# From residual rows to features between layers: VectorE block transposes and a DRAM scratch tile in place of TensorE transposes

## The chip, the cores and the metric

The kernel runs on one core of one Trainium2 chip. The metric is the device time of one execution in microseconds (us); the median of three runs is compared. The core has five engines with a queue of instructions each, which run at the same time: TensorE (PE; its weight loads are PEld), VectorE (DVE), ScalarE (ACT), GpSimd (POOL) and SyncE (SP). Sixteen DMA engines move data for the queues of SP, ACT and POOL.

## What is computed

A decoder trunk of four layers over a sequence of 256 rows of 2048 float32 values. Every layer normalizes the residual stream x, multiplies it with one wide input matrix, runs a mixer (latent attention, sparse attention, sliding window, latent attention) and a cross attention over a memory, gates the result and adds its output product to x.

```python
for i in range(DEPTH):                      # 4
    h = _rmsnorm(x, norm_in[i])             # x (1, 256, 2048)
    ...                                     # self_out, mq, gate from h @ w_in
    mem_out = _memory_attention(mq, mem_n @ w_mem_kv[i])
    y = jnp.concatenate([self_out, mem_out], axis=-1) * jax.nn.silu(gate)
    x = x + y @ w_out[i]
return _rmsnorm(x, final_norm)
```

## The kernel before, in words

The residual stream stays on chip as `xc`: four chunks `c` of 512 columns, each as two tiles `t` of 128 rows. Every product is made from float32r parts: a value is split into a high part (its rounding, made by ScalarE in `copy_act`, L74) and a low part (the rest, made by VectorE, L83), and three matmuls (high by high, high by low, low by high) are summed. Weights come by SP's DMAs into five tiles `wr`; `parts_of` splits them into `wh` and `wl`, of which there are three buffers each. So the split of a k-step (128 rows of a weight matrix) waits until the k-step three places earlier has been multiplied. I call these steps kv0 to kv15 in the product that opens layers 1 and 2 (`acc_kv`, 512 columns wide) and kva0 to kva15 in the one that opens layer 3 (`acc_kva`, 288 columns wide). Each step is six matmuls.

The last `w_out` of a layer (L1247) makes the four chunks one after the other: 24 matmuls (`acc_wo`), the addition into `xc` (L1251), and, where it is the last part, `nxt.chunk(c)` (L364) for the layer that follows. `chunk` makes `xT`, the features of this chunk on the partitions, in high and low parts, and the sums of squares of its rows (L234, ScalarE, into a scratch tile `junk`). In `to_features` (L211) TensorE turns four 128x128 pieces of each row tile into a PSUM bank (L215), VectorE multiplies them by the norm's weights into `xg` (L217), ScalarE and VectorE split `xg` into `xT`. Steps 4c to 4c+3 of the next layer's first product read chunk c of `xT`. There are three such boundaries: after layer 0 (some 935 to 970 us), after layer 1 and after layer 2 (some 1920 to 1955 us). Scratch tiles of 128x512 values (`tmp`: `xg`, `junk` and others) share four buffers.

The instructions of each engine run in one fixed order, which a scheduler with its own estimate of times sets when the program is built; a few are held in program order. POOL's queue carries the memory keys and values (`mv`, `mkT`), the bias tables and, in layers 0 and 1, one copy of a bias table at the first chunk of each of eight `w_out` calls (`not_before`, L175, a small copy named `tick`, then `table_copies`, L170).

Of the kernel before, what the change touches and what calls it, by code (L numbers as in the profile page):

```python
# [8 lines left out]
F32 = mybir.dt.float32  # L9
# [3 lines left out]
OP = mybir.AluOpType  # L13
AX = mybir.AxisListType

P = 128
# [29 lines left out]
def kernel(ctx: ExitStack, tc: tile.TileContext, a: dict, out: bass.AP,  # L46
                             kinds=(0, 1, 2, 0)):
    nc = tc.nc
# [3 lines left out]
    act = ctx.enter_context(tc.tile_pool(name="act", bufs=1))  # L52
    wk = ctx.enter_context(tc.tile_pool(name="wk", bufs=1))
    ps = ctx.enter_context(tc.tile_pool(name="ps", bufs=1, space=bass.MemoryType.PSUM))
    dr = ctx.enter_context(tc.tile_pool(name="dr", bufs=1, space=bass.MemoryType.DRAM))

    def misc(name, dt=F32):
        return ps.tile([P, 512], dt, name=name, tag="mp", bufs=4)

    def tmp(name, n=512, dt=F32):  # L60
        return wk.tile([P, n], dt, name=name, tag=f"t{n}", bufs=4)
# [5 lines left out]
    def f32(ap):  # L67
        return ap.bitcast(F32)
# [4 lines left out]
    def copy_act(o, i, scale=1.0):  # L73
        inst = nc.scalar.activation(o, i, AF.Copy, scale=scale)  # L74
        if pinned:
            tc.keep_in_program_order(inst)
# [4 lines left out]
    def split(hi, lo, src):  # L81
        copy_act(hi, src)
        nc.vector.tensor_sub(lo, src, f32(hi))  # L83


    xc = cst.tile([P, 4, 2, 512], F32, name="xc")
# [8 lines left out]
    gvec = cst.tile([P, P], F32, name="gvec")  # L95
    tc.keep_in_program_order(nc.scalar.dma_start(gvec, a["l_norms"]))

    class Features:

        def __init__(self, src, c):  # L100
            self.q = act.tile([P, 4, S], F32, name="ft", tag="pq", bufs=PQ)
            self.src = src[:, 4 * c:4 * c + 4, :]
# [108 lines left out]
    def to_features(dst, t, src, gcol, n=4):  # L211

        tp = misc("tp")
        for j in range(n):
            nc.tensor.transpose(tp[:, j * P:(j + 1) * P], src[:, j * P:(j + 1) * P], ident)  # L215
        xg = tmp("xg")
        nc.vector.tensor_mul(xg[:, :n * P].rearrange("p (j c) -> p j c", j=n),  # L217
                             tp[:, :n * P].rearrange("p (j c) -> p j c", j=n),
                             gvec[:, gcol:gcol + n][:, :, None].to_broadcast([P, n, P]))
        sl = slice(t * P, (t + 1) * P)  # L220
        g3 = xg[:, :n * P].rearrange("p (j c) -> p j c", j=n)
        split(dst[:, 0, :n, sl], dst[:, 1, :n, sl], g3)
# [9 lines left out]
    def square_sum(col, src):  # L232
        junk = tmp("junk")
        return nc.scalar.activation(junk[:, :src.shape[-1]], src, AF.Square, accum_out=col)  # L234
# [120 lines left out]
        nc.vector.tensor_add(dst[:, 1], z, pair[:, :, 1, :])  # L355


    class Norm:
        def __init__(self, layer):
            self.layer = layer  # L360
# [3 lines left out]
        def chunk(self, c):  # L364
            q = act.tile([P, 2, 4, S], F32R, name="xT", tag="xT", bufs=4)
            self.at.append(q)
            for t in range(2):
                src = xc[:, c, t, :]
                to_features(q, t, src, 64 + self.layer * 16 + c * 4)
                square_sum(self.ss[:, t * 4 + c:t * 4 + c + 1], src)  # L370

        def first_chunk(self, c):

# [958 lines left out]
```

## Time and profile before

| what | us |
|---|---|
| median of 3 runs | 2544.02 (2543.21 to 2544.23) |
| span of the profiled execution, first to last instruction | 2541.7 |
| TensorE busy in it | 2532.3 |
| VectorE, ScalarE, GpSimd busy | 1889.8, 1600.9, 95.6 |

The runs' times hold the span and the little that lies around it; the page gives the profiled execution's span only, 2.3 us under the median. Busy time is the time in which an engine had an instruction under way. A row of a timeline gives the start, the time until the end (rows of one kind in a row are merged), the engine, the line and the tiles, and in brackets how long the engine stood idle before and what ended that. The end of an instruction overlaps the start of the next, so starts are compared with starts.

### The profile page before, as it was taken

The numbers are of one execution on the slowest core, as the hardware profiler recorded it, in microseconds if no ns is written. First come the engines' busy times: TensorE is split into PE (matmuls) and PEld (weight loads), VectorE is DVE, ScalarE is ACT, GpSimd is POOL, SyncE is SP. The second block draws the span as 40 slices with busy tenths as digits, with TensorE's granted clock in tenths as the row PEclk, the third lists the DMA queues.
The fourth block names the chain that finished last, engine by engine and source line by source line (L and its number), as shares of the span: only waits on it lengthen the run. The fifth ranks groups of instructions, "written<-read, shape, count | busy, mean of one in ns | idle before, by whom it ended". The sixth has DMA issues, their size and how long they took to land.

```text
span 2541.7 us, 41606 instructions
## 1 busy us (share of the span) xinstructions
PE 2532.3 (100%) x14070; PEld 2185.3 (86%) x14070; DVE 1889.8 (74%) x3832; ACT 1600.9 (63%) x3291; POOL 95.6 (4%) x237
## 2 busy tenths in 40 slices
PE   9999999999999999999999999999999999999998
PEld 8888898888888889888888888888889888888887
DVE  6666667677777677988787777877867777777766
ACT  6556556566566566777666566667756666656655
POOL 1200000000000000000000000000000000000000
PEclk9999999999999999999999999999999999999999
DMA  9887777676667666766666565655656768676765
GB/s 315 260 262 257 248 215 236 169 191 176 187 194 207 195 197 188 219 190 175 190 187 182 174 216 175 182 176 177 195 158 178 225 189 218 194 194 183 222 173 183
DMA packets 479030, 511.67 MB, mean 201 GB/s; under 512 B 70720, under 2 KB 391616, under 8 KB 478176
## 3 DMA queue, kind: packets, MB, share of 16 engines
q1 hardware_dynamic: 462304, 451.82, 60.6%
q0 software_dynamic: 15792, 56.22, 7.0%
q8 instruction: 110, 1.80, 0.3%
q10 hardware_dynamic: 720, 0.98, 0.1%
q14 instruction: 104, 0.85, 0.1%
HBM read 483.67 MB, written 29.46 MB: 202 GB/s over the span
## 4 chain that ended last, share of the span: by engine, by line
PE 99%; DVE 1%; issue 0%; DMA 0%; ACT 0%; SPq 0%; ACTq 0%; DVEq 0%
PE acc_wo L292 20%; PE acc_g L313 14%; PE acc_g L317 7%; PE acc_mv L292 7%; PE acc_q L313 5%; PE acc_mq L313 5%; PE acc_mk L313 5%; PE acc_cq L313 4%; PE acc_qn L313 4%; PE acc_q L317 2%; PE acc_mq L317 2%; PE acc_mk L317 2%; PE acc_cq L317 2%; PE acc_qr L313 2%; PE acc_qn L317 2%; PE acc_va L292 2%
## 5 line engine op out<-in xcount | busy, mean ns | idle before, releaser
L74 ACT ACTIVATE wh<-wr 128x512 fp32r<-128x512 f32 (+1 forms) x1712 | 1062.6, 623 | 820.3 <-PE acc_g L313 147.3
L83 DVE TENSOR_TENSOR wl<-wr,wh 128x512 fp32r<-128x512 f32 (+1 forms) x1712 | 1155.1, 679 | 558.2 <-ACT wh L74 529.7
L313 PE MATMUL acc_g<-xT,wh 128*128 128x512 f32 x1536 | 483.8, 397 | 0.0
L292 PE MATMUL acc_wo<-wh,y 128*128 128x512 f32 x1504 | 473.2, 391 | 0.0
L317 PEld LDWEIGHTS acc_g<-xT,wl 128*128 128x128 f32 x1536 | 282.4, 188 | 63.0 <-DVE wl L83 1.1
L292 PEld LDWEIGHTS acc_wo<-wh,y 128*128 128x128 f32 x1504 | 282.5, 188 | 55.9
L317 PE MATMUL acc_g<-xT,wl 128*128 128x256 f32 x1536 | 304.8, 280 | 0.1
L292 PE MATMUL acc_wo<-wl,y 128*128 128x512 f32 x752 | 297.7, 396 | 0.0
L313 PEld LDWEIGHTS acc_g<-xT,wh 128*128 128x128 f32 x1536 | 235.4, 189 | 0.9
L292 PEld LDWEIGHTS acc_wo<-wl,y 128*128 128x128 f32 x752 | 141.3, 188 | 26.3
L313 PE MATMUL acc_q<-xT,wh 128*128 128x512 f32 x512 | 161.4, 396 | 0.0
L313 PE MATMUL acc_mq<-xT,wh 128*128 128x512 f32 x512 | 161.1, 396 | 0.0
L313 PE MATMUL acc_mk<-mT,wh 128*128 128x512 f32 x512 | 160.7, 395 | 0.0
L292 PE MATMUL acc_mv<-wh,mT 128*128 128x512 f32 x512 | 156.7, 390 | 0.0
L313 PE MATMUL acc_qn<-cT,wh 128*128 128x512 f32 x384 | 121.0, 396 | 0.0
L313 PE MATMUL acc_cq<-xT,wh 128*128 128x512 f32 x384 | 120.9, 396 | 0.0
L317 PEld LDWEIGHTS acc_mk<-mT,wl 128*128 128x128 f32 x512 | 95.8, 188 | 22.6 <-DVE wl L83 0.2
L1251 DVE TENSOR_TENSOR xc<-xc,acc_wo 128x1024 f32<-128x1024 f32 x92 | 112.0, 1218 | 2.6 <-PE acc_wo L292 2.3
L317 PEld LDWEIGHTS acc_q<-xT,wl 128*128 128x128 f32 x512 | 94.7, 188 | 22.2 <-issue 0.7
L317 PEld LDWEIGHTS acc_mq<-xT,wl 128*128 128x128 f32 x512 | 94.8, 188 | 21.7 <-issue 0.2
L292 PEld LDWEIGHTS acc_mv<-wh,mT 128*128 128x128 f32 x512 | 96.4, 189 | 19.8
L317 PE MATMUL acc_q<-xT,wl 128*128 128x256 f32 x512 | 102.2, 281 | 0.0
(332 smaller groups left out, 3830.7 us busy)
## 6 DMA issues: line engine op xcount, KB each, us to landing
wr<-in_w_out_dram SPq DMA_DIRECT2D x188, 512.0 KB, 3.7
wr<-in_w_in_a_dram SPq DMA_DIRECT2D x176, 512.0 KB, 4.3
wr<-in_w_mem_kv_dram SPq DMA_DIRECT2D x125, 512.0 KB, 4.5
wr<-in_w_in_b_dram SPq DMA_DIRECT2D x116, 512.0 KB, 3.6
wr<-in_w_in_c_dram SPq DMA_DIRECT2D x104, 512.0 KB, 3.5
wr<-in_w_uq_dram SPq DMA_DIRECT2D x288, 128.0 KB, 2.8
wr<-in_w_in_a_dram SPq DMA_DIRECT2D x32, 288.0 KB, 3.2
mv<-mv POOLq DMA_DIRECT2D x16, 512.0 KB, 5.9
```

The costliest lines, as they stand in the source:

```text
L74: inst = nc.scalar.activation(o, i, AF.Copy, scale=scale)
L83: nc.vector.tensor_sub(lo, src, f32(hi))
L292: nc.tensor.matmul(acc[t][:, :n], q[:, v, (s + k) % 4, t * P:(t + 1) * P], w_[:, :n], start=s + k == 0 and v == 0 and w_ is wh, stop=s + k ...
L313: nc.tensor.matmul(acc[j], wh[:, o:o + P], q[:, :, kt % 4, :], start=kt == 0, stop=False)
L317: nc.tensor.matmul(acc[j][:, 0, :], wl[:, o:o + P], q[:, 0, kt % 4, :], start=False, stop=kt == kts - 1)
L1251: nc.vector.tensor_add(xs, xs, acc)
```

## The change

`Norm.chunk` no longer calls `to_features`. VectorE transposes the 32x32 blocks of each row tile (`turn_blocks`, one instruction of 128x512 per tile) into scratch tiles `xet`; two DMAs on POOL's queue write them (256 KB each) to a DRAM tile `turned`; four more, one per group of 32 partitions, 128 KB each in runs of 512 bytes, read them back into `xt` with each feature's row whole. ScalarE and VectorE then make `xT` from `xt` in four pieces of 128x256, with the norm's weight as a factor per partition. The sums of squares come after that in program order. `xt` uses the buffers `big0` to `big3`. The first layer's features (`first_chunk`) and the latent mixer's use of `to_features` stay.

```diff
+    def turn_blocks(et, m0, src, step=1):
+        n = src.shape[-1] // P
+        nc.vector.transpose(et[:, :, m0:m0 + step * (n - 1) + 1:step, :],
+                            src.rearrange("p (m j c) -> p j m c", j=4, c=32))
+
+    def across(dst, ets):
+        u, n = len(ets), ets[0].shape[-1] // 4
+        d = dr.tile([u, 4, 32, 4, n], F32, name="turned", tag=f"turned{u * n}", bufs=4)
+        for t, et in enumerate(ets):
+            nc.gpsimd.dma_start(d[t].rearrange("i p j n -> (i p) (j n)"), et)
+        for j in range(4):
+            nc.gpsimd.dma_start(dst[32 * j:32 * j + 32].rearrange("p (i n) -> p i n", n=n),
+                                d[:, :, :, j, :].rearrange("t i p n -> p (t i) n"))
...
         def chunk(self, c):
             q = act.tile([P, 2, 4, S], F32R, name="xT", tag="xT", bufs=4)
             self.at.append(q)
+            ets = [tmp("xet") for t in range(2)]
             for t in range(2):
-                src = xc[:, c, t, :]
-                to_features(q, t, src, 64 + self.layer * 16 + c * 4)
-                square_sum(self.ss[:, t * 4 + c:t * 4 + c + 1], src)
+                turn_blocks(ets[t].rearrange("p (j m c) -> p j m c", j=4, m=4), 0, xc[:, c, t, :])
+            xt = act.tile([P, 8, 4, 32], F32, name="xt", tag=f"big{c}")
+            across(xt.rearrange("p u m c -> p (u m c)"), ets)
+            for k in range(4):
+                g = gvec[:, 64 + self.layer * 16 + c * 4 + k:][:, :1]
+                src = xt[:, :, k, :]
+                hi, lo = (q[:, v, k, :].rearrange("p (u c) -> p u c", c=32) for v in range(2))
+                copy_act(hi, src, scale=g)
+                nc.vector.scalar_tensor_tensor(lo, src, g, f32(hi), op0=OP.mult, op1=OP.subtract)
+            for t in range(2):
+                square_sum(self.ss[:, t * 4 + c:t * 4 + c + 1], xc[:, c, t, :])
```

The change moves instructions on ScalarE. At the boundary after layer 0 its queue had this order before, from the first square sums on (`wh<-wr` is the split of one k-step's weights, `xT<-xg` half of a chunk's features; the first row ends with the first k-step of the third chunk of `w_out`):

```order
L74 ACTIVATE wh<-wr 128x512 x20
L234 ACTIVATE junk,xss<-xc 128x512 x2
L74 ACTIVATE xT<-xg 128x4x128
L74 ACTIVATE wh<-wr 128x512
L74 ACTIVATE xT<-xg 128x4x128
L74 ACTIVATE wh<-wr 128x512 x3
```

These rows repeat for each of the four chunks, so that chunk 0 is split before the second k-step of the third chunk of `w_out`. In the changed kernel the same place reads, from the split of the third chunk's four k-steps of `w_out` on:

```order
L74 ACTIVATE wh<-wr 128x512 x4
L234 ACTIVATE junk,xss<-xc 128x512 x2
L74 ACTIVATE wh<-wr 128x512 x4
L234 ACTIVATE junk,xss<-xc 128x512 x2
L74 ACTIVATE wh<-wr 128x512 x3
L74 ACTIVATE xT<-xt,gvec 128x256 x4
L74 ACTIVATE wh<-wr 128x512
L74 ACTIVATE xT<-xt,gvec 128x256 x4
L74 ACTIVATE wh<-wr 128x512
L234 ACTIVATE junk,xss<-xc 128x512
L74 ACTIVATE wh<-wr 128x512
L234 ACTIVATE junk,xss<-xc 128x512
L74 ACTIVATE wh<-wr 128x512 x5
L74 ACTIVATE xT<-xt,gvec 128x256 x4
```

The first `x4` splits are the third chunk of `w_out`, the second `x4` the fourth, the `x3` after them kv0 to kv2. The first four pieces of `xT` now stand behind the split of kv2, the next four behind kv3, the third four behind kv6 to kv10; the last four, not shown, come behind kv11.

At the boundary after layer 2 ScalarE's queue in the changed kernel reads, from the split of the fourth chunk of `w_out` on (`wh<-wr 128x288` is the split of one step kva):

```order
L74 ACTIVATE wh<-wr 128x512 x4
L74 ACTIVATE xT<-xt,gvec 128x256 x4
L74 ACTIVATE wh<-wr 128x288
L234 ACTIVATE junk,xss<-xc 128x512
L74 ACTIVATE wh<-wr 128x288
L234 ACTIVATE junk,xss<-xc 128x512
L74 ACTIVATE wh<-wr 128x288 x3
L234 ACTIVATE junk,xss<-xc 128x512 x2
L74 ACTIVATE wh<-wr 128x288 x2
L74 ACTIVATE xT<-xt,gvec 128x256 x4
L74 ACTIVATE wh<-wr 128x288 x2
L74 ACTIVATE xT<-xt,gvec 128x256 x4
```

Chunk 0 stands ahead of kva0, chunk 1 behind kva6, chunk 2 behind kva8; the last four pieces, not shown, stand behind kva14.

POOL's queue had nothing between the first and the last of the following rows before. Now it reads, between the loads of memory keys and the small copy with which the next layer begins:

```order
L659 DMA mkr<-mkT_127 128x1024
L369 DMA turned<-xet 128x512 x2
L371 DMA xt<-turned 32x8x128 x4
L369 DMA turned<-xet 128x512 x4
L371 DMA xt<-turned 32x8x128 x8
L369 DMA turned<-xet 128x512 x2
L371 DMA xt<-turned 32x8x128 x4
L177 COPY tick<-kr 128x1
```

The writes of chunks 1 and 2 stand together ahead of the reads of both, and the writes of chunk 3 behind those reads; after layer 1 it is the same, with two small fills ahead of the last four reads. After layer 0 the writes and reads go by pairs of chunks (four writes, eight reads, twice), behind a copy of a bias table.

## Rows read from the trace of the kernel before

**Rows 1.** Page, parts 1, 2 and 4: busy time; clock by slice; chain by engine.

```profile
PE 2532.3 (100%) x14070; PEld 2185.3 (86%) x14070; DVE 1889.8 (74%) x3832; ACT 1600.9 (63%) x3291; POOL 95.6 (4%) x237
...
PEclk9999999999999999999999999999999999999999
...
PE 99%; DVE 1%; issue 0%; DMA 0%; ACT 0%; SPq 0%; ACTq 0%; DVEq 0%
```

**Rows 2.** Timeline of PE in `w_out`, without and with the transposes.

```profile
919.70 0.39 PE L292 MATMUL acc_wo<-wl,y 128*128 128x512 f32 x1
919.92 0.62 PE L292 MATMUL acc_wo<-wh,y 128*128 128x512 f32 x2
920.38 0.39 PE L292 MATMUL acc_wo<-wl,y 128*128 128x512 f32 x1
...
937.38 1.04 PE L215 MATMUL tp<-ident,xc 128*128 128x128 f32 x8
938.17 0.48 PE L292 MATMUL acc_wo<-wl,y 128*128 128x512 f32 x1
...
943.72 1.03 PE L215 MATMUL tp<-ident,xc 128*128 128x128 f32 x8
```

**Rows 3.** Timeline of PE in the first product of layer 3.

```profile
1944.09 0.69 PE L292 MATMUL acc_kva<-wh,xT 128*128 128x288 f32 x4
1944.61 0.42 PE L292 MATMUL acc_kva<-wl,xT 128*128 128x288 f32 x2
1944.87 0.69 PE L292 MATMUL acc_kva<-wh,xT 128*128 128x288 f32 x4
```

**Rows 4.** Timelines of DVE and ACT at the boundary after layer 0.

```profile
934.70 1.22 DVE L1251 TENSOR_TENSOR xc<-xc,acc_wo 128x1024 f32<-128x1024 f32 x1
...
938.62 0.68 DVE L83 TENSOR_TENSOR wl<-wr,wh 128x512 fp32r<-128x512 f32 x1
939.22 0.68 DVE L217 TENSOR_TENSOR xg<-tp,gvec 128x512 f32<-128x512 f32 x1
...
935.99 0.63 ACT L74 ACTIVATE wh<-wr 128x512 fp32r<-128x512 f32 x1 [0.73 <-PE acc_wo L292]
966.34 0.42 ACT L74 ACTIVATE dgr<-dg 128x256 fp32r<-128x256 f32 x1 [0.26 <-DVE dg L203]
```

**Rows 5.** Line 229, the product of 128x256 by a column on DVE.

```profile
L229 DVE SCALAR_TENSOR_TENSOR xT<-ft,gvec,xT x16: 473/478/481, 108.5 to 252.6; 128x256 fp32r<-128x256 f32 x16
```

**Rows 6.** POOL's issue of `sw` and `bm`, ns min/median/max, and the landing of `bm`.

```profile
L1230 POOL DMA_DIRECT2D sw<-hl x16: 536/536/547, 2050.5 to 2273.8; - x16
...
L1019 POOL DMA_DIRECT2D bm<-tab x16: 617/626/653, 797.3 to 1776.5; - x16
...
DMA to landing us min/median/max: 3.7/5.0/7.7
```

**Rows 7.** DMA view: POOL's DMAs, KB each, median us from issue to landing.

```profile
mvr<-mv POOLq DMA_DIRECT2D x16, 512.0 KB, 5.9
mkr<-mkT POOLq DMA_DIRECT2D x16, 512.0 KB, 7.9
...
tab<-flat POOLq DMA_DIRECT2D x8, 768.0 KB, 6.1
...
sw<-hl POOLq DMA_DIRECT2D x16, 256.0 KB, 3.7
...
hl<-in_w_out_dram POOLq DMA_DIRECT2D x16, 128.0 KB, 3.6
```

**Rows 8.** POOL at the boundary after layer 0; landing of `hl` and `sw` together.

```profile
935.98 0.58 POOL L177 COPY tick<-xc 128x1 f32<-128x1 f32 x1 [19.37 <-DVE xc L1251]
936.50 0.54 POOL L173 DMA_DIRECT2D tab<-flat  x1
...
DMA to landing us min/median/max: 2.6/3.7/9.2
```

**Rows 9.** Windows: us, busy time by engine (PE, PEld, DVE, ACT, POOL), clock, DMA share, GB/s.

```profile
937.00:953.00 16.00, 16.00 (x85) 13.49 (x84) 14.70 (x23) 12.45 (x28) 0.04 (x1) 1.00 0.74 220
...
1032.00:1034.00 2.00, 2.00 (x15) 1.82 (x15) 1.57 (x5) 1.88 (x7) 0.00 (x0) 1.00 1.10 381
...
1930.00:1950.00 20.00, 20.00 (x130) 18.39 (x130) 18.89 (x42) 15.09 (x36) 0.00 (x0) 1.00 0.41 112
...
2536.00:2541.00 5.00, 0.00 (x0) 0.00 (x0) 0.92 (x3) 1.08 (x3) 0.00 (x0) 0.50 0.57 210
```

**Rows 10.** Page, part 5: weight loads of `w_out`, busy us, mean ns, idle us before.

```profile
L292 PEld LDWEIGHTS acc_wo<-wh,y 128*128 128x128 f32 x1504 | 282.5, 188 | 55.9
```

## The prediction

> **What bounds the kernel now.** I read the page first: TensorE is busy 100% of the span at the full clock, and the chain that ended last is TensorE for 99% [rows 1]. So a microsecond taken from TensorE's queue is a microsecond won, and one in which it waits is lost. Next the timeline of TensorE at the boundaries between layers, where the transposes stand; then those of VectorE, ScalarE and POOL there, and the order of the changed kernel.
>
> **What goes.** In `w_out` three matmuls start in 0.68 us (919.70 to 920.38), so a chunk's 24 take 8 x 0.68 = 5.44 us. With eight transposes a chunk takes 6.34 (937.38 to 943.72) [rows 2]. A group thus costs 0.90: 0.79 of its own and 0.11 for the weight loads behind it. There are 12 groups (4 chunks, 3 boundaries): **-10.8 us**, all on the path.
>
> **What comes: a longer way.** I count from the end of a chunk's matmuls. The addition lasts 1.22, a next instruction may start 0.09 earlier [rows 4]; one weight split (0.60) stands ahead of the transposes. No 32x32 transpose is in this trace. Its price lies between an instruction of half the size, 0.42, and one of twice the size, 1.22; I take the 0.68 of a VectorE instruction of the same size, 0.60 to the next [rows 4]. So both scratch tiles are ready at 0.1 + 1.13 + 0.60 + 0.60 + 0.68 = 3.1. Two writes are issued, each when its tile is ready (0.54 each [rows 6]). The second lands 3.7 later, as `sw` does, which is also 256 KB out of 128 partitions [rows 7]: 6.9. Only then are the four reads issued, at the 0.63 of `bm`, which has the same 256 pieces [rows 6]: the last at 8.8. For its landing I take 4.2, between `hl` (same bytes, 3.6 [rows 7]) and `bm` (twice the bytes, 5.0 [rows 6]): 13.0. One piece on ScalarE (0.42 [rows 4]) and one on VectorE (0.48 [rows 5]): **13.9 us**, of which TensorE does none.
>
> What hides it: the other three chunks of `w_out`, 3 x 5.44 = 16.3 us, since kv0 comes after them and each later chunk is wanted 5.44 later. After layers 0 and 1 that covers 13.9. After layer 2 it does not: a step kva lasts 0.78 [rows 3], four steps 3.1, so chunk c has only 16.3 - 2.3c: 14.0, 11.7 and 9.3 for chunks 1, 2 and 3. POOL's order makes it worse. It waits for chunk 2's transposes before it issues chunk 1's reads, and issues chunk 3's writes only behind the eight reads of chunks 1 and 2. By that queue the eighth read leaves at some 4.1 after the end of `w_out`, chunk 3's second write at 5.2, lands at 8.9, and with reads (1.9 + 4.2) and pieces (0.9) chunk 3 is there at 15.9 to 16.3. Wanted at 9.3: TensorE waits **7 us** in sum after layer 2.
>
> **What comes: work queued in the wrong place.** ScalarE and VectorE run strictly in order, and splits have three buffers. So a piece of `xT` that stands behind the split of step n starts only after step n-3 has been multiplied and that split is done: 0.1 + 0.55 on ScalarE, then 0.42. In the order shown, after layer 0 chunk 0 stands behind kv2, whose buffer comes free when `w_out` ends; kv0 wants it at that very moment. Its low part stands behind the last addition too: 0.1 + 1.13 + 0.60 + 0.48 = 2.3 after that end, wanted at 0.45. So 1.9, even if the data has long landed. Chunk 2 stands behind kv10, which waits for kv7, and kv8 wants it: again 2.1. The second chunk's square sums wait for a scratch buffer, thus for chunk 0's write, which lies behind the 768 KB copy of a table (landing after 6.1) [rows 7, 8]; ScalarE leads TensorE by 1.4 us there (its 0.73 us pause before each split [rows 4], twice) and is held about 2.5, so 1 more. Sum after layer 0: **5**. After layer 1 chunk 3 stands behind kv14, and kv12 wants it (1.6), and low parts crowded ahead of the splits of kv1, kv2 and kv5 cost some 2: **3.6**. After layer 2 chunk 1 stands behind kva6, and kva4 wants it; that wait is part of the 7.
>
> A weight load (0.19 [rows 10]) that runs beside the matmul before it stands bare behind each such wait: about 11 waits, **2 us**. VectorE's load changes little: two transposes and four products (1.2 + 1.6) replace two multiplications and two subtractions (2.4), and it was not the bound.
>
> **Traffic.** Per chunk 0.5 MiB goes out and comes back, 1 MiB in 5.44 us: 190 GB/s on top of 220 in the 16 us after 937 and of 112 in the 20 after 1930. The most that moved in any window I looked at is 381, at a share of 1.10 [rows 9]. So after layer 0 the engines are full and landings longer than the medians; with the chain's one write and one read 0.7 longer each, I add **4** over the three boundaries.
>
> **Sum:** 5 + 3.6 + 7 + 2 + 4 = 21.6 of waits, less 10.8: +10.8. The page's span is 2541.7 and its runs' median 2544.0; the 2.3 around the span stay. **2555 us**, +0.42%. The bounds of the unknown landings: at the shortest seen, 2.6 [rows 8] for a write and a read, only the waits by order remain, some 15, net +4 (2548). At the 5.9 and more of POOL's bursts of 512 KB [rows 7] the chain is 13.9 + 2.2 + 1.7 = 17.8 us, no boundary covers it, and with writes that queue behind reads each boundary loses some 9 more: 48 of waits, net +38 (2582).
>
> The Trainium skill (DMA: Bandwidth & Descriptors, Anatomy of one DMA) gives a DMA of POOL's queue 2.0 us and its bytes by 436 GB/s; by that, an estimate, a write would take 2.6, a read 2.3, and the sum would be the +4 above. This trace does not agree: 3.7 and 3.6 for the same sizes [rows 7].
>
> **Rivals.**
> - *All of it hides* (2533): the landings are short and the pieces are ready whenever their engine reaches them, so TensorE keeps only the -10.8. For: 13.9 is less than 16.3 at two boundaries. Against: the order, which holds pieces back whatever the DMA does, and kva's short steps. It decides at waits under 11 in sum. Chance 0.08.
> - *Only the order counts* (2548): landings near 3 us. For: the shortest in the trace. Against: the medians, and the added traffic. Chance 0.17; about half of it lies within 5 us of before.
> - *The queue clogs* (2570 to 2590): each write and read lands in 5 to 6 us, since 400 GB/s is wanted and 381 is the most seen; reads wait for writes on one queue, and weights may come late too. Chance 0.15.
> - *The clock falls* (2568): the granted clock is 1.00 in every window in which TensorE works, and 0.50, its 1.2 GHz level, only in one where it has had nothing for 5 us [rows 9]. A wait after layer 2 of 3 us or more may let it fall in mid-kernel. The sixteen steps kva (16 x 0.78 = 12.5 us) at half the clock would cost 12.5 more. Against: the waits come in pieces, with matmuls between. Chance 0.08. The Trainium skill (TensorE: Matmul & The Clock Gate, The HAM clock gate) warns that idleness drops the engine to half its rate; no stretch of this trace tests that between matmuls.
>
> **How the numbers follow.** Forecast 0.52, rivals 0.08, 0.17, 0.15, 0.08. The range reaches from just below the waits by order alone to the bound of long landings: 2546 to 2582, which leaves out the case of full gain and what is above. 0.2%, about 5 us, is what a measurement of this kernel can tell from no change. Faster: the first rival, 0.08. Within: half of the second and the low edge of the forecast, 0.17. Slower: the rest, 0.75.
>
> **What would show it.** In the new profile the rows of L215 on `xc` are gone, and the chunks of `w_out` follow each other every 5.44 us. TensorE has idle time before `acc_kv` and `acc_kva` of some 5, 4 and 8 us at the three boundaries, put down to `xT` on ScalarE or VectorE, most of it before kv0, kv8, kv12, kva4 and kva12. Writes land in 3.7 to 4.5, reads in 4 to 5. I am wrong if TensorE's idle time stays under 10 us (the order holds less than I think), if the most of it comes after layers 0 and 1 (then traffic, not kva's pace, decides), or if the clock leaves 1.00.

## The result, and the profile after

The changed kernel took **2561.31 us** (median of 4 runs, 2560.23 to 2567.22) beside 2543.69 for the kernel before (4 runs, 2543.21 to 2544.23): a ratio of 1.0074, 95% interval 1.0060 to 1.0088. It is slower by 17.6 us, clear of the 0.2% that can be told from no change, on the side the prediction gave 0.75, and 6.3 us above the predicted 2555.0. The profiled execution took 2560.23, its span is 2558.4, 16.7 longer than the span before.

The page of the changed kernel (busy time, the chain), to be laid beside [rows 1]:

```profile
PE 2532.2 (99%) x13974; PEld 2179.9 (85%) x13974; DVE 1895.5 (74%) x3856; ACT 1606.3 (63%) x3315; POOL 136.9 (5%) x309
...
PE 96%; DMA 2%; POOL 1%; DVE 1%; issue 0%; ACT 0%; ACTq 0%; POOLq 0%; DVEq 0%
```

TensorE lost its 96 transposes, which occupied 12 x 0.79 = 9.5 us, and yet its busy time is the same to 0.1 us. So its other matmuls were busy 9.4 us longer, and idle time came on top (2558.4 less 2532.2 is 26.2, before it was 9.4: 16.8 more). The chain, 99% TensorE before, now runs for 4% through DMA, POOL and VectorE.

Where in the program? Three landmarks on TensorE enclose the three boundaries: the first matmul of `acc_cq` and the first of `acc_iq` (after layer 0 lies between), the first and the last of `acc_q` (after layer 1), the last of `acc_q` and the last of `acc_cq` (after layer 2). Rows of the tile view, of before:

```profile
L317 PE MATMUL acc_cq<-xT,wl x384: 274/277/368, 385.1 to 2034.6; 128*128 128x256 f32 x192
L340 PE MATMUL acc_iq<-xT,wl x144: 250/272/358, 976.8 to 1020.1; 128*128 128x192 f32 x128, 128*80 128x256 f32 x16
L317 PE MATMUL acc_q<-xT,wl x512: 274/277/386, 1071.7 to 1790.9; 128*128 128x256 f32 x171
```

and of the changed kernel:

```profile
L317 PE MATMUL acc_cq<-xT,wl x384: 273/278/368, 386.0 to 2051.5; 128*128 128x256 f32 x192
L340 PE MATMUL acc_iq<-xT,wl x144: 250/272/357, 983.3 to 1026.6; 128*128 128x192 f32 x128, 128*80 128x256 f32 x16
L317 PE MATMUL acc_q<-xT,wl x512: 273/278/387, 1078.2 to 1799.8; 128*128 128x256 f32 x171
```

From 385.1 to 976.8 are 591.7 us before and 597.3 after: **+5.6** at the first boundary. In the same way **+2.4** at the second (719.2 and 721.6) and **+8.0** at the third (243.7 and 251.7). Outside of them the two kernels differ by 0.9 us at most. The same three differences, from one profile each, are given below for the experiments.

The removal itself is there. The chunks of `w_out` followed each other every 6.34 us [rows 2]; now VectorE's additions behind the first three, from its timeline after layer 1, stand 5.44 apart:

```profile
1458.32 1.22 DVE L1277 TENSOR_TENSOR xc<-xc,acc_wo 128x1024 f32<-128x1024 f32 x1
...
1463.76 1.22 DVE L1277 TENSOR_TENSOR xc<-xc,acc_wo 128x1024 f32<-128x1024 f32 x1
...
1469.20 1.22 DVE L1277 TENSOR_TENSOR xc<-xc,acc_wo 128x1024 f32<-128x1024 f32 x1
```

What came in its place, in the view of TensorE's waits (us in total, times, longest):

```profile
PE acc_kv L292 <- ACT xT L74: 7.5, 4, 2.6
PE acc_kva L292 <- ACT xT L74: 6.7, 2, 3.8
PE acc_kv L292 <- DVE wl L83: 1.2, 1, 1.2
```

Before, none of these rows existed. With two small ones (0.5) that is 15.9 us of idle time: 5.1 at the first boundary (2.50 ahead of kv0, 2.59 ahead of kv8), 3.6 at the second (1.22, 1.27, 1.12) and 6.7 at the third (2.89 ahead of kva4, 3.77 ahead of kva12). The steps of the longer way, from the tile view, with the time from issue to landing as min, median, max of `xet` (the writes) and of `xt` (the reads):

```profile
L361 DVE STREAM_TRANSPOSE xet<-xc x24: 667/686/705, 937.4 to 1949.8; 128x512 f32<-128x512 f32 x24
...
DMA to landing us min/median/max: 2.4/5.8/7.3
...
L371 POOL DMA_DIRECT2D xt<-turned x48: 582/584/617, 946.1 to 1960.2; - x48
...
DMA to landing us min/median/max: 2.6/4.9/7.6
```

A block transpose takes 0.69, where 0.68 had been taken. A write lands in 5.8 and a read in 4.9, where 3.7 and 4.2 had been taken [rows 6, 7]. And TensorE's clock left its full rate behind the longer waits. The timeline of TensorE behind the last of them (a step kva is two rows, four matmuls by `wh` and two by `wl`):

```profile
1965.54 1.24 PE L292 MATMUL acc_kva<-wh,xT 128*128 128x288 f32 x4 [3.77 <-ACT xT L74]
...
1967.06 1.16 PE L292 MATMUL acc_kva<-wh,xT 128*128 128x288 f32 x4
...
1968.50 1.16 PE L292 MATMUL acc_kva<-wh,xT 128*128 128x288 f32 x4
...
1969.94 0.70 PE L292 MATMUL acc_kva<-wh,xT 128*128 128x288 f32 x4
```

Three steps take 1.52, 1.44 and 1.44 instead of 0.78 [rows 3], a loss of 2.06; then the pace is back. Behind the wait at kva4 three steps lose 1.86 (4.20 us from 1952.78 to 1956.98), behind that at kv0 ten matmuls lose 2.0 (4.27 from 955.49 to 959.76, 2.27 at full rate). The mean granted clock of the three stretches, from the windows view, is 0.60, 0.59 and 0.61: for most of each the engine was at 0.50, its 1.2 GHz level. So 5.9 us of the 9.4 by which the matmuls were busy longer are slow steps behind a wait. By an estimate from these means the clock alone accounts for some 5.1 of them (0.40 of 4.27, 0.41 of 4.20 and 0.39 of 4.40 us); weight loads that stand bare there are the likely remainder. What is left of the 9.4, 3.5 us, lies in many small places, and so does the 0.9 of idle time in pauses too short to be listed. The removal counts for 1.3 more in a sum with 10.8 than it does in busy time (9.5). Together these small terms are 5.7.

The account: 15.9 idle + 5.9 slow steps + 5.7 small, less 10.8, is the +16.7 of the span.

### The profile page after: what moved, and what is told of

Same layout as the page of the kernel before. It is cut to its first block, busy times and chain, and to the rows that moved or that the text cites. A ratio compares the mean times of both kernels' runs of the same rounds, so it can differ in the third digit from the quotient of the medians.

```text
span 2558.4 us, 41633 instructions
## 1 busy us (share of the span) xinstructions
PE 2532.2 (99%) x13974; PEld 2179.9 (85%) x13974; DVE 1895.5 (74%) x3856; ACT 1606.3 (63%) x3315; POOL 136.9 (5%) x309
## 4 chain that ended last, share of the span: by engine, by line
PE 96%; DMA 2%; POOL 1%; DVE 1%; issue 0%; ACT 0%; ACTq 0%; POOLq 0%; DVEq 0%
PE acc_wo L292 19%; PE acc_g L313 14%; PE acc_g L317 7%; PE acc_mv L292 7%; PE acc_q L313 5%; PE acc_mq L313 5%; PE acc_mk L313 5%; PE acc_cq L313 3%; PE acc_qn L313 3%; PE acc_q L317 2%; PE acc_mq L317 2%; PE acc_mk L317 2%; PE acc_cq L317 2%; PE acc_qr L313 2%; PE acc_qn L317 2%; PE acc_va L292 2%
## 5 line engine op out<-in xcount | busy, mean ns | idle before, releaser
L317 PEld LDWEIGHTS acc_mq<-xT,wl 128*128 128x128 f32 x512 | 94.9, 188 | 21.6 <-issue 0.2
```

Source lines behind the costliest of these rows:

```text
L317: nc.tensor.matmul(acc[j][:, 0, :], wl[:, o:o + P], q[:, 0, kt % 4, :], start=False, stop=kt == kts - 1)
```

## The experiments

Differences at the three boundaries against the kernel before, in us, from one profile each as worked out above. At the boundary after layer 1, where e3 leaves the changed kernel as it is, the two profiles differ by 2.0 us, so between kernels that go through DRAM a difference of that size tells nothing. Without that way the boundaries repeat far better (e5 and e10: within 0.1).

| kernel | median us | ratio, 95% interval | 1st | 2nd | 3rd |
|---|---|---|---|---|---|
| changed | 2561.31 | 1.0074 (1.0060 to 1.0088) | +5.6 | +2.4 | +8.0 |
| e1 | 2548.57 | 1.0018 (1.0009 to 1.0027) | +1.5 | +1.5 | +1.8 |
| e2 | 2565.85 | 1.0087 (1.0072 to 1.0102) | +8.1 | +10.4 | +6.3 |
| e3 | 2561.83 | 1.0072 (1.0057 to 1.0087) | +5.3 | +4.4 | +7.0 |
| e4 | 2563.35 | 1.0073 (1.0056 to 1.0089) | +7.7 | +6.2 | +8.4 |
| e5 | 2545.55 | 1.0004 (0.9995 to 1.0014) | +0.5 | +0.4 | +0.2 |
| e6 | 2542.93 | 0.9995 (0.9985 to 1.0004) | -0.7 | -0.7 | 0.0 |
| e7 | 2559.48 | 1.0058 (1.0043 to 1.0073) | +4.1 | +3.8 | +7.2 |
| e8 | 2557.85 | 1.0053 (1.0038 to 1.0068) | +7.4 | +4.0 | +5.1 |
| e10 | 2545.13 | 1.0004 (0.9994 to 1.0014) | +0.4 | +0.4 | +0.2 |
| e12 | 2554.85 | 1.0044 (1.0027 to 1.0061) | +3.1 | -0.4 | +6.4 |

The kernel before, run beside them on the same chip, had medians of 2544.01 (e1 to e4), 2544.41 (e5 to e8), 2544.15 (e9 to e11) and 2544.14 (e12).

**e1: no way through DRAM.** In `chunk`:

```diff
-            xt = act.tile([P, 8, 4, 32], F32, name="xt", tag=f"big{c}")
-            across(xt.rearrange("p u m c -> p (u m c)"), ets)
...
+                for t in range(2):
+                    src = ets[t].rearrange("p (j m c) -> p j m c", j=4, m=4)[:, :, k, :]
...
```

> The changed kernel without the scratch tile in DRAM: the 32x32 transposes stay, and ScalarE and VectorE read their result where it lies (so the blocks never reach the other partitions, and a piece is 128x128 instead of 128x256). If the waits of the changed kernel come from the landings of the writes and reads, TensorE's idle time at the three boundaries falls from 15.9 us to under 4, its clock stays at 1.00, and the time is 2533 to 2537. If they come from the work of the two other engines, from where the pieces stand in their order, or from the transposes on VectorE, idle time of 8 us or more stays and the time is 2545 or more.

It took 2548.57: 13 us less than the changed kernel, but still 4.6 more than before, so the rival's outcome, by number. The idle time of 8.1 us is put down to `wl` throughout, and half of it lies in `w_out`:

```profile
PE acc_wo L292 <- DVE wl L83: 4.2, 6, 1.1
PE acc_kv L292 <- DVE wl L83: 2.6, 2, 1.3
PE acc_kva L292 <- DVE wl L83: 1.3, 2, 0.9
```

Not only the transfers cost something. Even with the data on the spot, the 10.8 us do not come out.

**e5: no transpose at all, and e6: transposes in place with the large pieces.** These two split e1's finding. e5 makes the pieces straight from `xc`:

```diff
-            ets = [tmp("xet") for t in range(2)]
...
-                src = xt[:, :, k, :]
+                src = xc[:, c, :, k * P:(k + 1) * P]
```

> No transpose at all between layers: the pieces of xT are taken straight from the stream, untransposed (so xT holds the wrong axis), four of 128x256 on ScalarE and four on VectorE for a chunk as in the changed kernel. VectorE then has 4 splits x 0.60, an addition of 1.13 and pieces of 4 x 0.48: 5.4 us for a chunk of 5.44. If the transposes taken from TensorE are worth 0.90 a group, the time is 2532 to 2535 (-10.8). If VectorE stands close behind TensorE as the next bound, part of it is lost and the time is 2537 to 2541.

e6 keeps VectorE's block transposes and has pieces of 128x256 as in the changed kernel:

```diff
-            ets = [tmp("xet") for t in range(2)]
+            xt = act.tile([P, 2, 4, 4, 32], F32, name="xt", tag=f"big{c}")
             for t in range(2):
-                turn_blocks(ets[t].rearrange("p (j m c) -> p j m c", j=4, m=4), 0, xc[:, c, t, :])
-            xt = act.tile([P, 8, 4, 32], F32, name="xt", tag=f"big{c}")
-            across(xt.rearrange("p u m c -> p (u m c)"), ets)
+                turn_blocks(xt[:, t], 0, xc[:, c, t, :])
...
```

> The kernel of e1 (32x32 transposes, no way through DRAM) with pieces of 128x256 as in the changed kernel, 1.9 us on VectorE for a chunk instead of 2.2. With the two transposes (1.2) VectorE has 6.6 us of work in a chunk of 5.44 of TensorE. If VectorE is the bound behind TensorE, idle time of about 1.5 us a boundary stays, put down to wl, and the time is 2544 to 2548. If it was the small pieces alone that kept e1 from its gain, the time is 2533 to 2538.

Both results lie outside what either theory gave. e5, which does nothing in place of the transposes, took 2545.55: **taking 96 transposes off the engine that is busy 100% of the span won nothing that can be measured.** e6, which adds VectorE's block transposes and has more work on VectorE than e5, took 2542.93, somewhat less (its two waits after layer 1 are 0.85 and 0.57, at the same kind of place). That speaks against the amount of VectorE's work. The timeline of ScalarE in e5 after layer 0 shows one half of what it is (pieces, square sums, then three splits in a row without a pause between them):

```profile
936.33 0.63 ACT L74 ACTIVATE wh<-wr 128x512 fp32r<-128x512 f32 x1 [0.73 <-PE acc_wo L292]
936.87 1.69 ACT L74 ACTIVATE xT<-xc,gvec 128x256 fp32r<-128x256 f32 x4
938.47 0.62 ACT L234 ACTIVATE junk<-xc 128x512 f32<-128x512 f32 x1
...
939.08 0.62 ACT L234 ACTIVATE junk<-xc 128x512 f32<-128x512 f32 x1
...
939.69 1.65 ACT L74 ACTIVATE wh<-wr 128x512 fp32r<-128x512 f32 x3
```

and TensorE's timeline what follows from it:

```profile
942.29 0.50 PE L292 MATMUL acc_wo<-wl,y 128*128 128x512 f32 x1 [1.42 <-DVE wl L83]
...
955.15 0.50 PE L292 MATMUL acc_kv<-wl,xT 128*128 128x512 f32 x1 [1.42 <-DVE wl L83]
```

Four pieces and two square sums hold ScalarE for 2.8 us (936.87 to 939.69). With three buffers the splits lead TensorE by 1.4 us, about one step of six matmuls (1.36). In its rhythm of 1.36 a step the next split would have started at 937.69; it starts at 939.69, 2.0 us late, and the lead is gone. The kernel before had one piece, then one split, then one piece, in this place:

```profile
939.11 0.61 ACT L74 ACTIVATE xT<-xg 128x512 fp32r<-128x512 f32 x1
939.66 0.63 ACT L74 ACTIVATE wh<-wr 128x512 fp32r<-128x512 f32 x1
940.20 0.62 ACT L74 ACTIVATE xT<-xg 128x512 fp32r<-128x512 f32 x1
```

**e10: VectorE relieved.**

```diff
-                nc.vector.scalar_tensor_tensor(lo, src, g, f32(hi), op0=OP.mult, op1=OP.subtract)
+                nc.gpsimd.tensor_copy(lo, f32(hi))
```

> The kernel of e5 with the low pieces made by a copy on POOL (so they hold the wrong numbers), which takes 1.9 us a chunk from VectorE; buffers as before. If VectorE's amount of work is the next bound behind TensorE, the time falls to 2534 to 2538. If the stretch of 2.8 us on ScalarE ahead of the splits is what TensorE waits for, it stays at 2543 to 2546.

2545.13, as e5, and TensorE's two waits after layer 1 are 1.42 each, as in e5. With 1.9 us a chunk taken from VectorE nothing moves, so the amount of VectorE's work is not the cause in e5. The rows of the three engines around the first of these waits show what is:

```profile
1458.07 1.65 ACT L74 ACTIVATE wh<-wr 128x512 fp32r<-128x512 f32 x3
...
1458.78 1.22 DVE L1272 TENSOR_TENSOR xc<-xc,acc_wo 128x1024 f32<-128x1024 f32 x1 [2.72 <-PE acc_wo L292]
1459.92 2.09 DVE L83 TENSOR_TENSOR wl<-wr,wh 128x512 fp32r<-128x512 f32 x3
...
1460.66 0.50 PE L292 MATMUL acc_wo<-wl,y 128*128 128x512 f32 x1 [1.42 <-DVE wl L83]
```

The profile names `wl`, and `wl` does not wait for ScalarE here: the high half of the split is done by 1458.7. In VectorE's order the low half stands behind the addition into `xc`, and that waits, with VectorE idle for 2.72 us, until TensorE has finished the chunk. So two things meet. The row of pieces on ScalarE brings the first split of the next chunk so late that its low half is made only behind the addition, and the addition, which needs TensorE's last matmul of the chunk, adds over 1.2 us (1458.7 to 1459.92). All five waits of 1.42 in e5, and the five in e10, have this form. In e6 and e1 the low half that TensorE waits longest for in `w_out` also stands behind the addition on VectorE, with low pieces between them, and its high half had been done for over a microsecond; VectorE has no pause there, so for these two the amount of its work is not ruled out. No run moved the addition alone, so how the loss divides between ScalarE's row and VectorE's order is not shown.

**e9 and e11: one more buffer for the splits.**

```diff
-PQ, AUX, WR, PT, WARM = 5, 4, 5, 4, 11
+PQ, AUX, WR, PT, WARM = 5, 4, 4, 4, 11
...
-        wh = wp.tile([P, 512], F32R, name="wh", tag="wh", bufs=3)
+        wh = wp.tile([P, 512], F32R, name="wh", tag="wh", bufs=4)
```

(`wl` alike.)

> The kernel of e5 with four buffers instead of three for each half of the weight splits (and four instead of five for the raw weights, to make room). In e5 ScalarE has four pieces and two square sums, 2.8 us, in one stretch ahead of the next splits, and TensorE then waits 1.42 for wl: the splits lead it by only about 1.4 us. If the short lead ate the 10.8 us, one more buffer (1.36 us of steps) takes most of it back: 2534 to 2538. If it is the amount of work on VectorE and ScalarE, the buffer changes nothing: 2544 to 2547. Fewer raw buffers could also make weights late: above 2547.

> The changed kernel with the same four buffers for each half of the splits and four for the raw weights. If the waits of the changed kernel are mostly late data (e6, which has no way through DRAM, is 18 us faster), the lead helps only the waits put down to wl and the pieces' place behind the splits: 2555 to 2559. If the lead decides in the changed kernel too, it falls by as much as e9 falls against e5, to about 2550. With the pieces standing behind more splits it may also get no better: 2560.

As tests of the whole time both told nothing (e9 met its open outcome above 2547, e11 none of its three): 2608.02 (1.0245, 1.0226 to 1.0263) and 2629.83 (1.0337, 1.0321 to 1.0353), because the loss came elsewhere. The largest wait of either is `acc_va` for `kn` (20.5 and 20.8 us in total), in the attention layers; whether the raw buffer that was given up or the splits that run further ahead make it was not tried apart. At a boundary alone e9 can be read. From the matmul ahead of the last `w_out` to the last of kv after layer 0 it takes 44.6 us (956.5 to 1001.1) where e5 takes 47.8 (929.1 to 976.9) and the kernel before 47.4 (928.8 to 976.2); 192 matmuls every 0.227 would take 43.5. The same row of 2.8 us stands on ScalarE there, and of the two waits of 1.42 one of 0.49 is left. So with a longer lead the removal does pay at that boundary: 2.8 us against the kernel before, of the 3.6 that four groups of transposes cost. This is one boundary of one profile in a kernel that is slower elsewhere. e11 was too disturbed to say more.

**e4: pieces ahead of the splits.**

```diff
+                if name in ("kv", "kva") and (s + k) % 4 == 0 and (s + k) // 4 in pieces:
+                    on_act, on_dve = pieces.pop((s + k) // 4)
+                    with tc.issue_after(on_act), tc.issue_after(on_dve):
+                        wh, wl = parts_of(wr, k * n, n)
...
```

> The changed kernel with the pieces of chunk c put ahead of the weight split of step 4c on ScalarE and VectorE, instead of up to three splits behind it. If the place in the order holds the pieces back though their data are there, as my sum has it for kv0, kv8 and kv12, the waits after layers 0 and 1 shrink by 4 to 6 us and the time is 2555 to 2557. If the data are not there, the pieces wait at their new place instead, the splits behind them too, and the time is 2560 to 2565.

2563.35, no better, and the waits changed their name, not their size:

```profile
PE acc_kva L299 <- ACT wh L74: 7.0, 2, 4.8
PE acc_kv L299 <- ACT wh L74: 6.2, 4, 2.5
PE acc_kv L299 <- DVE wl L84: 4.6, 4, 2.4
```

ScalarE now stood at the pieces of chunk 0 for 2.55 us (at 955.72) and at those of chunk 1 for 1.25, each time for a read, with the splits behind. The data were not there. The changed kernel's own timeline of ScalarE says the same for kv0 (its first row below) and kv8 (a pause of 1.36 ahead of the pieces, put down to the same DMA), and the opposite for kv12 after layer 1:

```profile
954.92 1.71 ACT L74 ACTIVATE xT<-xt,gvec 128x256 fp32r<-128x256 f32 x4 [1.08 <-DMA xt<-turned]
...
1495.60 0.63 ACT L74 ACTIVATE wh<-wr 128x512 fp32r<-128x512 f32 x1 [0.87 <-PE acc_kv L292]
1496.14 1.69 ACT L74 ACTIVATE xT<-xt,gvec 128x256 fp32r<-128x256 f32 x4
```

There the pieces follow the split of kv14 without a pause for data, and that split had waited for TensorE. So the prediction's reading, that pieces whose data had landed were held by their place, falls for kv0 and kv8 and holds for kv12 after layer 1.

**e3: the clock kept up.**

```diff
+    def fill(acc, name, k, wh, n):
+        for _ in range({("kv", 1, 0): 10, ("kva", 3, 12): 26}.get((name, state[0], k), 0)):
+            nc.tensor.matmul(acc[:64, :n], zeror, wh[:, :n], start=k == 0, stop=k == 0)
...
```

> The changed kernel with matmuls by a tile of zeros in front of two of the steps that wait: 10 before kv0 after layer 0 (2.3 us beside a wait of 2.5) and 26 before kva12 after layer 2 (3.5 us beside 3.8). They add nothing to the result and should end when the data come. If the clock falls because TensorE has nothing to do in those waits, it stays at 1.00 behind both, and the half-rate steps go: about 1.6 us behind kv0 (3.3 us at half) and 2 us behind kva12 (three steps of 1.44 instead of 0.78), so 2557 to 2558. If the clock falls for another reason, or its fall costs nothing, the time stays at 2561 or gets longer.

At the two filled waits the clock did as the first theory says. Windows of e3 behind the filled wait at kv0, behind the wait at kva4 that was left empty (4.14 us here), and behind the filled one at kva12:

```profile
957.00:959.00 2.00, 2.00 (x10) 1.39 (x9) 2.00 (x5) 0.63 (x1) 1.08 (x2) 1.00 0.95 230
...
1956.00:1958.00 2.00, 2.00 (x9) 2.00 (x10) 1.85 (x8) 1.03 (x3) 0.00 (x0) 0.53 0.99 328
...
1968.00:1970.00 2.00, 2.00 (x16) 2.00 (x17) 1.64 (x5) 1.43 (x4) 0.00 (x0) 1.00 0.00 0
```

The same stretch of the changed kernel behind kv0:

```profile
957.00:959.00 2.00, 2.00 (x6) 1.57 (x5) 1.64 (x4) 0.57 (x1) 1.08 (x2) 0.50 1.03 234
```

Ten matmuls are under way in these 2 us instead of six. So at these two places the clock falls behind the wait when TensorE has nothing to do in it, and stays up when matmuls that add nothing fill it. That it would give back 3.6 us of the whole is not shown: the median is 2561.83. At the two boundaries this profile is 0.3 and 1.0 us better, with a wait at kva4 that is 1.25 longer than in the changed kernel's profile; and after layer 1, where nothing was filled, the wait ahead of kv4 is 2.16 instead of 1.27, and the clock fell to 0.50 behind it (window 1485.2 to 1488.4), which it had not done in the changed kernel. How much of the 5.9 a steady clock would return to the whole time stays open.

**e2: all transfers on SP's queue, and e7: the writes alone.**

```diff
-            nc.gpsimd.dma_start(d[t].rearrange("i p j n -> (i p) (j n)"), et)
+            nc.sync.dma_start(d[t].rearrange("i p j n -> (i p) (j n)"), et)
```

(e2 does the same with the reads.)

> The same writes and reads issued from SP's queue, between the weights, instead of POOL's. If a landing on POOL's queue is long because of that queue (5.8 us for a write, 4.9 for a read, where SP's queue lands 512 KB of weights in 3.5 to 4.4), a write lands in about 3.3 and a read in about 2.9, the waits after layer 2 mostly go, and the time is 2540 to 2548. If the landings are long because 400 GB/s are asked for, they stay at 5 us or more on any queue, weights come late behind them as well, and the time is 2560 or more.

> The changed kernel with its writes issued from SP's queue and its reads from POOL's, so that no write stands behind the reads of other chunks. By the theory that POOL's queue, where writes wait behind reads and reads behind writes, makes up most of the lateness: writes land in about 4.0 as in e2, reads in 4.9, nothing waits for a landing in front of the weights, and the time is 2548 to 2555. If the landings themselves and VectorE make the loss, it is 2558 or more.

Of e2 the first half came true in the main: in its DMA view a write lands in 4.0 and a read in 2.6 (3.3 and 2.9 were expected), beside the same weights, against 5.8 and 4.9 on POOL's queue. That is not the queue alone: in e2 two writes or four reads are under way at a time, in the changed kernel up to four writes or seven reads, and the two were not tried apart. The time got worse all the same, 2565.85, where 2540 to 2548 belonged to short landings. SP's queue after layer 1, from its timeline (start, duration):

```profile
1462.37 0.93 SPq L369 DMA_DIRECT2D turned<-xet  x2
...
1466.44 1.80 SPq L371 DMA_DIRECT2D xt<-turned  x4
...
1475.87 1.80 SPq L371 DMA_DIRECT2D xt<-turned  x4
...
1484.14 1.80 SPq L371 DMA_DIRECT2D xt<-turned  x4
...
1492.18 1.80 SPq L371 DMA_DIRECT2D xt<-turned  x4
```

One queue in order: a chunk's reads wait for its writes to land, and the next chunk's writes stand behind those reads, with a weight load between. So a chunk's reads leave every 8.0 to 9.4 us, and TensorE has one ready every 5.44. ScalarE waits up to 3.40 for a read with the splits behind it, and the profile puts TensorE's waits down to `wh`.

e7 took 2559.48, which is the second theory's outcome: with the writes out of POOL's queue the median is 1.8 us lower, and the intervals of the two kernels overlap (1.0043 to 1.0073 and 1.0060 to 1.0088), so a gain is not shown. Its writes land in 4.5, its reads in 5.1.

**e8: two chunks of four.**

```diff
+            if c >= 2:
+                for t in range(2):
+                    src = xc[:, c, t, :]
+                    to_features(q, t, src, 64 + self.layer * 16 + c * 4)
...
```

> The new way for chunks 0 and 1 alone, TensorE's transposes for chunks 2 and 3, at all three boundaries. It gives up half of the removal (-5.4 stays). If the late chunks (2 and 3 after layers 0 and 1, 1 to 3 after layer 2) and the crowd of transfers make the loss, chunks 0 and 1 are there in time, 2 to 4 us of waits stay, and the time is 2540 to 2544. If every chunk that goes through DRAM brings its own wait, it is 2550 or more.

2557.85: half of the transfers, three quarters of the loss (13.4 against 17.6 us, of which 5.4 is the half of the removal that it gives up). The second theory holds. POOL's queue after layer 1 shows why chunk 1 is late although only two chunks are sent:

```profile
1467.86 2.35 POOL L371 DMA_DIRECT2D xt<-turned  x4 [3.86 <-DMA turned<-xet]
1470.20 1.13 POOL L369 DMA_DIRECT2D turned<-xet  x2
```

Its writes stand behind chunk 0's reads and leave at 1470.20; its own reads leave at 1478.51, after 7.18 us of waiting for them, and its pieces start at 1486.04. That is the 2.76 by which TensorE waits ahead of kv4.

**e12: step by step.** On e7's queues:

```diff
+                    with one_by_one():
+                        wh, wl = parts_of(wr, k * n, n)
+                    with one_by_one():
+                        after_split(s + k)
```

(`after_split` makes the one piece that step n multiplies, `one_by_one` issues a block behind the one before it on ScalarE and VectorE.)

> The kernel of e7 (writes from SP's queue) with the pieces of a chunk no longer four in a row: behind the weight split of step n stands the one piece that step n multiplies, then the split of step n+1, on ScalarE and on VectorE. If rows of four pieces ahead of the splits make a good part of the loss, as e5 and e10 show for the kernel without a way, the waits put down to wh and wl (about 9 us in e7) mostly go and the time is 2552 to 2556. If the data are what is late, they wait for the first piece of a chunk instead and the time is 2558 to 2562; if holding the splits back behind late pieces costs more than the rows of four did, 2563 or more.

2554.85, 4.6 less than e7 (its four runs, 2552.62 to 2555.61, all lie below the four of e7, 2556.28 to 2560.81, from another chip; by the ratios to the kernel before on the same chip it is 3.6 less, and those intervals overlap, 1.0027 to 1.0061 and 1.0043 to 1.0073) and the lowest median of the kernels that go through DRAM. The largest waits:

```profile
PE acc_kva L310 <- ACT xT L74: 5.2, 2, 4.4
PE acc_kv L310 <- ACT xT L74: 2.0, 5, 0.9
PE acc_wo L310 <- ACT wh L74: 1.3, 1, 1.3
```

Of the 10 us that e7 had at the boundaries put down to `wh` and `wl`, 1.5 are left. The edit changes two things at once, the length of the rows and the place of each piece, so the gain belongs to both. After layer 1 the boundary is 0.4 us shorter than before, in this one profile, which tells nothing; after layer 2 it is still 6.4 longer, 4.36 of it one wait ahead of kva12. What remains is late data, where the steps are short. Of the kernels that leave nothing out, none beats the kernel before.

## Why the prediction was nearly right, point by point

- **"What goes: -10.8."** It holds in the changed kernel: the chunks of `w_out` after layer 1 take 5.44 instead of 6.34, and the account closes with the whole 10.8, since the pieces come so late there that `w_out` has only 0.5 us of waits. As a rule it fails. "So a microsecond taken from TensorE's queue is a microsecond won" would give the 10.8 to e5 and e6, and they win none that can be told: there the pieces come early, ScalarE's row of four takes up the 1.4 us by which the splits lead, and the low half of a split stands behind the addition on VectorE. The sum counted a piece at 0.42 and looked for crowded splits in the product behind `w_out`, and inside it only at the square sums. VectorE's amount of work "was not the bound": e10 shows it for the form of e5, and nothing in the changed kernel speaks against it.
- **Block transposes, 0.68:** measured 0.69.
- **Landings, 3.7 and 4.2, plus 4 us for traffic.** Mis-sized: 5.8 and 4.9. The rows of `sw` and `hl` [rows 7] come from the last layer, where the code sends one tile at a time over POOL's queue; here six to twelve DMAs follow each other. The prediction put the risk down to traffic; in e2, with the same bytes on another queue and fewer of them under way at a time, they are 4.0 and 2.6. The way through DRAM as a whole, from e6 to the changed kernel, costs 17 to 20 us (2561.31 - 2542.93 = 18.4; by the landmarks 16.0 + 1.4 = 17.4; by the ratios 20).
- **Waits of "5, 4 and 8".** Measured idle: 5.1, 3.6 and 6.7, ahead of kv0, kv8, kva4 and kva12 as forecast. The sum was close for a mixed reason. After layer 0 the two places were explained by order with the data landed, and the data were not there. After layer 1 two of the three waits have the forecast form: kv12 by its place (1.12, 1.6 taken), kv1 by low parts crowded ahead of its split (1.22, some 2 taken), though those low parts had waited for late data themselves; the third, ahead of kv4 (1.27), is late data. After layer 2 it was POOL's order and late data, as forecast (6.7, 7 taken). Rows of four and the places of the pieces have a part in these waits: without them e12 is some 4 us shorter than e7, with intervals that overlap.
- **"Bare weight loads, 2":** with the other small terms, 5.7.
- **The clock** was left out of the sum and stood as a rival at +12.5 with 0.08. It happened, in three pieces of some 2 us, 5.9 with the loads that stand bare there; and the wait of 3 us or more that the rival asked for was not needed, 2.50 ahead of kv0 did it. The Trainium skill (TensorE: Matmul & The Clock Gate, The HAM clock gate) warns that idleness drops the engine to half its rate; this trace agrees for three of the four waits of 2.50 us and more, with 0.50 behind them, and not for the 2.59 at kv8; e3 shows the two levels with and without work in the wait.
- **Rivals.** "Only the order counts" and "all of it hides" are out. "The queue clogs" had the landings right (5 to 6 us) and the price too high, since after layers 1 and 2 chunk 0's way still fits under `w_out`. What e5 shows was among none of them.

The forecast of +10.8 became +16.7 in the profile's span: the waits were 3.7 less than the 19.6 in the sum (its 21.6 without the bare loads), the slow steps 5.9 more, the small terms 3.7 more. That errors of both signs met is luck, and the range held 36 us. Two of the prediction's signs of being wrong came true while its time held: the clock left 1.00, and 9.2 of the 15.9 us of idle time lie after layers 0 and 1. The second was ill chosen, since the forecast itself put 9 of 17 there; its meaning, that landings and not only kva's pace decide, is what the runs show.

## What to carry to other kernels

Before pricing what leaves the bounding engine, look at how far its feeders run ahead of it (here 1.4 us), whether the new code puts a longer row of work ahead of them, and whether what they make next then stands behind something that waits for the bounding engine itself: a kernel that takes the work away and puts nothing in its place is the first experiment to run. A trip through DRAM on one in-order queue costs two landings, and the next chunk's write stands behind this chunk's reads; count it at the landing times of a loaded queue, not of a quiet one. Pieces that are needed one per step did better here when they were issued one per step (e12).

## What the runs showed of the hardware that was not expected

- In mid-kernel the granted clock fell to 0.50 behind waits of TensorE of 2.50 (kv0), 2.89 and 3.77 us, and the matmuls behind them lost some 2 us each time. Behind the 2.59 at kv8 it stayed at 1.00, as behind those of 1.12 to 1.27, and in e5 behind five of 1.42; in e12 it fell to 0.50 behind one of 1.33 in `w_out` (window 948.0 to 951.3). So the length of a wait alone does not tell. Matmuls by a tile of zeros in a wait kept it at 1.00 (e3).
- The same writes and reads beside the same weights landed in 4.0 and 2.6 us from SP's queue (e2), where fewer were under way at a time, and in 5.8 and 4.9 from POOL's.
- A 32x32 block transpose of 128x512 fp32 values on VectorE lasts 0.69 us, as long as a subtraction of that size.
